# Two groups of six hidden chunks by seven products for eight in the first block, and the rotary tables built early and kept in DRAM

## The chip, the cores and the metric

The kernel runs on one core of one Trainium2 chip. The metric is the device time in microseconds (us) of one execution. The engines are named as in the profile: PE is TensorE (PEld its weight loads), DVE VectorE, ACT ScalarE, POOL GpSimd, SP SyncE, which here only issues DMAs.

## The reference

One encoder layer in float32: 512 tokens, model width 1024, hidden width 2816 (22 chunks of 128).

```python
def swiglu(h, w_in, w_out):
    gate, up = jnp.split(h @ w_in, 2, axis=-1)
    return (jax.nn.silu(gate) * up) @ w_out
# Per layer:
#   x += 1/2 * g1 * SwiGLU_1(mod(RMSNorm(x)))
#   x += g2 * W_out( sig(gA) * W_A(WindowGQA+sink) + sig(gB) * W_B(DiffAttn) )
#   x += 1/2 * g3 * SwiGLU_2(mod(RMSNorm(x)))
# shift, scale and g of each line: adaLN columns computed from c
```

The queries and keys of both mixers are rotated by the cosines and sines of `positions * inv_freq` (`rope_tables`). The change concerns the first line (SwiGLU_1, "the first block"), the step from it to the second, and the place where the rotary tables are made.

## The kernel before

**Products.** The residual x lies transposed, as eight row tiles of 128 model columns by 512 tokens (`x_78` to `x_85`, row tiles 0 to 7). Each float32 operand is split into a high part and a low part, and each product is three matmuls (high x high, high x low, low x high; `mm3`, L179 to L181, or `two`, L463 to L465). A weight is loaded into a `raw` buffer (a ring of five), ScalarE casts its high part, VectorE subtracts to get its low part (`split_from`, L195), and both stand in one of five places of a ring until TensorE has used them.

**Seven for eight.** Where the kernel works "by sevens", a product of two matrices that are each cut two by two is made from seven smaller products of sums of the parts, in place of eight. A `Unit` holds such a set: its seven are called s1, a11, a12, s2, s3, s4, a22, and its products have 256 columns (half of the tokens). Its sums of weights are made by DMA accumulations on POOL's queue or by VectorE, and its results are combined by VectorE (L541 to L551). The first block's incoming products go by sevens from hidden pair `PLAIN` = 3 on.

**Outgoing products of the first block.** The 22 hidden chunks leave in sets given by `CHUNKS`: 0 to 5 plain, 6 to 11 by sevens (`SEVEN = (1,)`, two units of `out_unit1`, updates at L1001), 12 to 15 plain, 16 to 21 plain and final. A plain set (`Out1`) goes row tile by row tile: for each, its chunks' products of 512 columns add up in one bank, and VectorE adds the bank, times the gate column g1, to x (L1073). In the final set ScalarE then squares the new x and VectorE adds the square to a sum (`Norm.add`, L309 and L315), for the root mean square of the next norm.

**The boundary.** The last `LAST_1` = 4 row tiles of the final set are made by halves of the tokens (256 columns) in `boundary`, from L386 on: first all four first halves, each followed by its update and `Norm.add`; then the second halves, and among them, at steps that `TO_MIX` counts, the sums of squares of the first half (`Norm.close`, two groups of small matmuls at L348: first of the running sum, then of the last row tile's square alone), the norm's factor and its spread over partitions (L327, L328, L337), and the input of the gates (L359, L360, L368). Then come the first gates' products for the first half, the second half's sums of squares (L348 again), and so on. A step is one chunk's three matmuls; `TO_MIX[0]` = 4 steps of the second half stand before the close, `TO_MIX[2]` = 2 steps of the gates before the second half's sums.

**What sets the order.** Each engine runs its instructions in one written order. On PE, DVE and ACT in the boundary that order is the one in which the code is written, but for what is told to stand behind another instruction (`issue_after`) or is put in by the scheduler where it sees room. SP and POOL run their DMA issues in written order. Modulation columns (`column`, on DVE L288) are spread over the items of the first block by rates (`AHEAD_OF`, `BEHIND`, and 0 in the sevens groups' own items), and loads of 0.5 MB come with them.

**The rotary tables.** A row of parameters is loaded beside the unit behind the sevens group (`load_row`, `by[-1]`). Behind the first block's last items the angles are computed (L1224 to L1241), then the sines; sixteen products (L1268 to L1271) make eight tables: those of the first mixer (`late`) are written to DRAM, those of the second (`soon`) stay in a raw buffer.

**The gates' weights.** `load_split` loads three gate weights of 128x1024 into raw buffers (L222); their casts on ACT and their low parts on DVE (128x1024, L195) fall into the boundary.

## Time and profile before

| | us |
|---|---|
| median of 3 runs | 1031.42 |
| lowest, highest | 1030.89, 1032.16 |
| the profiled execution | 1030.95 |
| its span | 1029.2 |
| PE busy in it | 1023.9 |
| DVE busy | 804.4 |
| ACT busy | 593.8 |
| POOL busy | 168.7 |

A row of a timeline gives the start, the duration, the engine, the line, the operation, what is written and read, and the shape; in brackets stands the idle time just before it and what ended it. A row of the groups of waits gives who waited for what: us in total, times, the longest. A row of busy time by window gives the window, its width, and then the busy time of PE, PEld, DVE, ACT and POOL with their instruction counts, the granted clock of TensorE, the share of the DMA engines' time and GB/s. Buffer numbers are left out of the profile's names. The profile's line numbers are those of the kernel before; in the order of instructions of the changed kernel the same code has the numbers L180 to L182 (products), L196 (splits), L228 (low parts of the gates' weights), L391 (update of a half), L314 and L320 (square and its addition), L332 (norm's factor), L1154 (update of a plain set).

### The profile page before, as it was taken

What the parts mean: (1) busy time and instruction counts of PE and PEld (TensorE: products, weight loads), DVE (VectorE), ACT (ScalarE), POOL (GpSimd) and SP (SyncE); (2) the same over time, 40 slices, a digit from 0 to 9 for tenths busy, and PEclk for the clock granted to TensorE, in tenths of its full rate; (3) what the DMA queues carried; (4) which work ended last, traced back from release to release, by engine and by line L of the source; (5) the groups of instructions that cost most, each with busy time, mean ns of one, the idle gap of its engine ahead of it and who ended that gap; (6) DMA issues with size and microseconds to landing.
All of it is one profiled execution on the core that took longest, in us unless ns stands there. A gap on an engine that the chain in (4) does not pass through costs nothing.

```text
span 1029.2 us, 19174 instructions
## 1 busy us (share of the span) xinstructions
PE 1023.9 (99%) x7454; PEld 950.0 (92%) x7454; DVE 804.4 (78%) x1508; ACT 593.8 (58%) x1040; POOL 168.7 (16%) x197
## 2 busy tenths in 40 slices
PE   9999999999999999999999999999999999999998
PEld 7889899999998988899878888989999999999998
DVE  7887868778878879859772688976898777877877
ACT  6755336553454533768795866534877546655553
POOL 1101011211100100543322101001112112212210
PEclk9999999999999999999999999999999999999999
DMA  9968888998957369696637935974498998999874
GB/s 361 371 192 202 292 220 207 222 227 259 244 153 245 134 259 409 220 274 136 165 83 193 275 120 176 344 243 106 101 237 196 242 231 209 224 223 219 208 156 114
DMA packets 71388, 223.57 MB, mean 217 GB/s; under 512 B 8576, under 2 KB 13312, under 8 KB 71296
## 3 DMA queue, kind: packets, MB, share of 16 engines
q1 hardware_dynamic: 47808, 146.52, 39.4%
q0 software_dynamic: 20352, 71.32, 37.5%
q10 hardware_dynamic: 3136, 4.51, 1.2%
q8 instruction: 58, 0.95, 0.4%
q14 instruction: 34, 0.28, 0.1%
HBM read 212.09 MB, written 10.23 MB: 216 GB/s over the span
## 4 chain that ended last, share of the span: by engine, by line
PE 96%; DVE 2%; ACT 1%; issue 0%; DVEq 0%; ACTq 0%
PE acc L463 7%; PE acc L465 7%; PE acc L464 7%; PE sc L463 7%; PE sc L465 7%; PE sc L464 7%; PE acc L179 5%; PE acc L180 5%; PE acc L181 5%; PE sc L180 4%; PE sc L179 4%; PE sc L181 4%; PE tp L1445 2%; PE sc L192 2%; PE acc L714 2%; PE sc L714 2%
## 5 line engine op out<-in xcount | busy, mean ns | idle before, releaser
L195 ACT CAST high<-raw 128x1024 fp32r<-128x1024 f32 (+2 forms) x176 | 159.0, 914 | 137.7 <-PE acc L464 32.4
L195 DVE TENSOR_TENSOR low<-raw,high 128x1024 fp32r<-128x1024 f32 (+2 forms) x176 | 183.7, 1051 | 42.7 <-ACT high L195 41.7
L463 PE MATMUL acc<-b,high 128*128 128x256 f32 x542 | 150.2, 277 | 0.0
L464 PE MATMUL acc<-b,high 128*128 128x256 f32 x542 | 149.9, 277 | 0.1
L465 PE MATMUL acc<-b,low 128*128 128x256 f32 x542 | 149.9, 277 | 0.0
L464 PE MATMUL sc<-b,high 128*128 128x256 f32 x534 | 147.5, 276 | 0.0
L463 PE MATMUL sc<-b,high 128*128 128x256 f32 x534 | 147.5, 276 | 0.0
L465 PE MATMUL sc<-b,low 128*128 128x256 f32 x534 | 147.5, 276 | 0.0
L195 DVE TENSOR_TENSOR low<-u,high 128x1024 fp32r<-128x1024 f32 (+1 forms) x79 | 93.3, 1181 | 26.7 <-ACT high L195 25.7
L195 ACT CAST high<-u 128x1024 fp32r<-128x1024 f32 (+1 forms) x79 | 80.4, 1019 | 50.0 <-PE sc L464 14.3
L463 PEld LDWEIGHTS acc<-b,high 128*128 128x128 f32 x542 | 101.8, 188 | 0.6 <-DVE f L543 0.3
L464 PEld LDWEIGHTS acc<-b,high 128*128 128x128 f32 x542 | 101.8, 188 | 0.4 <-DVE b L2033 0.3
L465 PEld LDWEIGHTS acc<-b,low 128*128 128x128 f32 x542 | 101.8, 188 | 0.1
L463 PEld LDWEIGHTS sc<-b,high 128*128 128x128 f32 x534 | 100.3, 188 | 0.0
L465 PEld LDWEIGHTS sc<-b,low 128*128 128x128 f32 x534 | 100.3, 188 | 0.0
L464 PEld LDWEIGHTS sc<-b,high 128*128 128x128 f32 x534 | 100.2, 188 | 0.0
L179 PE MATMUL acc<-b,high 128*128 128x512 f32 (+1 forms) x240 | 89.1, 371 | 0.0
L181 PE MATMUL acc<-b,low 128*128 128x512 f32 (+1 forms) x240 | 86.5, 361 | 0.0
L180 PE MATMUL acc<-b,high 128*128 128x512 f32 (+1 forms) x240 | 86.5, 360 | 0.0
L179 PE MATMUL sc<-b,high 128*128 128x512 f32 (+1 forms) x224 | 78.7, 351 | 0.0
L180 PE MATMUL sc<-b,high 128*128 128x512 f32 (+1 forms) x224 | 78.5, 350 | 0.0
L181 PE MATMUL sc<-b,low 128*128 128x512 f32 (+1 forms) x224 | 78.4, 350 | 0.0
(411 smaller groups left out, 2739.1 us busy)
## 6 DMA issues: line engine op xcount, KB each, us to landing
u<-w_mod SPq DMA_DIRECT2D x38, 512.0 KB, 8.4
b<-w_mod SPq DMA_DIRECT2D x32, 512.0 KB, 5.1
raw<-w2i SPq DMA_DIRECT2D x31, 512.0 KB, 5.7
u<-w2i POOLq DMA_DIRECT2D x31, 512.0 KB, 7.0
raw<-w1u SPq DMA_DIRECT2D x24, 512.0 KB, 7.6
u<-w1u POOLq DMA_DIRECT2D x24, 512.0 KB, 8.3
raw<-w_gate SPq DMA_DIRECT2D x16, 512.0 KB, 5.8
low<-w_gate POOLq DMA_DIRECT2D x13, 512.0 KB, 7.2
```

Of the source, the lines that this page charges most:

```text
L179: PE.matmul(out, wh, xh, start=first, stop=False)
L180: PE.matmul(out, wh, xl, start=False, stop=False)
L181: PE.matmul(out, wl, xh, start=False, stop=last)
L192: last = PE.matmul(out, of[j][a], of[j][b], start=i == 0, stop=i == 2).ins
L195: last = S.copy(hi, src), V.tensor_tensor(lo, src, f(hi), ALU.subtract)
L463: PE.matmul(out, wh[:, s], xh, start=first and j == 0, stop=False, skip_group_check=True)
L464: PE.matmul(out, wh[:, s], xl, start=False, stop=False, skip_group_check=True)
L465: PE.matmul(out, wl[:, s], xh, start=False, stop=last and j == 1, skip_group_check=True)
L714: PE.matmul(out1[i][:, r], w[:, i * P : (i + 1) * P], h[:, r], start=first and r.start == 0, stop=last and r.stop == T, skip_group_check=True,
L1445: PE.transpose(tp[:, j * P : (j + 1) * P], src, ident)
```

## The change

The chunks 12 to 17 leave as a second group by sevens, in place of four of them in a plain set and two in the final set, and the final set has four chunks. Five row tiles instead of four are made by halves in the boundary. Modulation columns get a rate in the sevens groups' items (`AMONG`), and places of the ring of weights are moved (`KICKS_1`). One step of the gates more stands before the second half's sums. The row is loaded at row tile 0 of the first plain set, and `tables()` is called at its row tile 1; both halves of the tables go to DRAM, issued by ACT, and `soon` is loaded back by SP ahead of the gates' weights. The low parts of the gates' weights are no longer issued with their casts: they stand in a list, `gate_lows`, and `boundary` issues one behind each update but the first.

```diff
@@ -106,11 +106,11 @@
 
 MIX_ASIDES = 0, 0, 0, 0, 0, 0, FIRST, ASIDE
 
-CHUNKS = (range(0, 6), range(6, 12), range(12, 16), range(16, 22))
-PLAIN, LAST_1 = 3, 4
-
-
-SEVEN, AHEAD_OF, BEHIND = (1,), (0.75, 0.4), (0.5, 0.25)
+CHUNKS = (range(0, 6), range(6, 12), range(12, 18), range(18, 22))
+PLAIN, LAST_1 = 3, 5
+
+
+SEVEN, AHEAD_OF, BEHIND, AMONG = (1, 2), (0.75, 0.4), (0.5, 0.25), (0.18, 0.18)
 
 
 EARLY, NEXT, LATER = 3, 3, 4
@@ -127,9 +127,10 @@
 
 BY_DMA = (5, 7)
 
-KICKS = (3, 5, 7)
-
-TO_MIX = (4, 13, 2, 2, 4, 2, 1)
+ROW_AT, TABLES_AT = 0, 1
+KICKS, KICKS_1 = (3, 5, 7), {6: "s3", 7: "s3", 9: "s3", 10: "s2"}
+
+TO_MIX = (4, 13, 3, 2, 4, 2, 1)
 TO_FFN2 = (3, 1, 2, 2, 3, 2, 1)
 
 PARTS = (range(0, 4), range(4, 8), range(8, 11))
@@ -213,14 +214,18 @@
         for i in [i for i in holders if holders[i] == holder]:
             del holders[i]
 
-    def load_split(src, n=1024, spare=False, aside=0):
+    def load_split(src, n=1024, spare=False, aside=0, due=None):
         raw = sbuf("raw", [P, 1024], F32, RAW)
         if spare:
             hi, lo = (u4().rearrange("p a b -> p (a b)") for _ in range(2))
         else:
             hi, lo = high_low(aside=aside)
         nc.sync.dma_start(raw[:, 0:n], src)
-        split_from(hi[:, 0:n], lo[:, 0:n], raw[:, 0:n])
+        if due is None:
+            split_from(hi[:, 0:n], lo[:, 0:n], raw[:, 0:n])
+        else:
+            S.copy(hi, raw)
+            due.append(lambda: V.tensor_tensor(lo, raw, f(hi), ALU.subtract))
         return hi, lo
 
     HALVES = (slice(0, 2 * P), slice(2 * P, T))
@@ -374,7 +379,7 @@
         hl = [t[2 + c // 4][:, c % 4, :] for c in range(NC)]
         return hh, hl
 
-    def boundary(parts, g, norm, sc, sh, hh, hl, into, ahead, at):
+    def boundary(parts, g, norm, sc, sh, hh, hl, into, ahead, at, due=()):
 
 
 
@@ -383,8 +388,9 @@
 
         def update(m, po, r):
             xr = x[m][:, r]
-            V.scalar_tensor_tensor(xr, po, modv[g][:, m : m + 1], xr, ALU.mult, ALU.add)
+            end = V.scalar_tensor_tensor(xr, po, modv[g][:, m : m + 1], xr, ALU.mult, ALU.add).ins
             norm.add(m, r)
+            return end
 
         def run(steps, n=None):
             for i, _ in enumerate(steps):
@@ -405,10 +411,13 @@
             yield
 
         with tc.manual_schedule(engines=BOUND):
-            for m, products in parts:
+            for i, (m, products) in enumerate(parts):
                 po = bank("sc")[:, 0 : 2 * P]
                 run(products(po, ra))
-                update(m, po, ra)
+                end = update(m, po, ra)
+                if due and i > 0:
+                    with tc.issue_after(end):
+                        due.pop(0)()
             n = 0
             for m, products in parts:
                 po = bank("sc")[:, 0 : 2 * P]
@@ -903,12 +912,14 @@
         u.p, u.in_order = p, ("s2", "s4")
         if p - 1 in by_sevens:
             u.in_order = ("s1", "s2", "s3", "s4", "a22")
-            if p not in by_sevens:
+            if 2 * p in [CHUNKS[i].stop for i in SEVEN]:
                 u.MAKE = dict(Unit.MAKE, s4=1)
         if p == PLAIN:
             u.asides = {"s1": FIRST}
         elif 2 * p in [CHUNKS[i].stop for i in range(len(CHUNKS) - 1) if i not in SEVEN] or p == PLAIN + 1:
             u.asides = {"s2": FIRST}
+        if p in KICKS_1:
+            u.asides = {KICKS_1[p]: FIRST}
         return u
 
     act = {}
@@ -1011,9 +1022,79 @@
     def load_row():
         rows.append(u4(F32).rearrange("p a b -> p (a b)")[:, 0:NROW])
         nc.sync.dma_start(rows[0], a["row"].partition_broadcast(P))
-        rows.append(split[1])
+
+    NF = HD // 2
+    table_scr, soon_scr = (tc.dram_tile([P, 1024], F32, name=nm) for nm in ("table_scr", "soon_scr"))
+    sink = keep([P, 8], "sink")
+
+    def four(t):
+        return [t[:, i * 2 * P : (i + 1) * 2 * P].rearrange("p (t d) -> p t d", t=NT) for i in range(4)]
+
+    def tables():
+        row = rows[0]
...
+        late = u4(F32).rearrange("p a b -> p (a b)")
+        soon = u4(F32).rearrange("p a b -> p (a b)")
+
...
+        S.dma_start(table_scr, late)
+        S.dma_start(soon_scr, soon)
...
+    by[-2] = lambda: (iter(()), 0, tables)
 
     def eighth(u):
         def steps():
@@ -1162,18 +1243,16 @@
                 for m in range(2):
                     item1(out, m, ks=range(len(chunks) - 2, len(chunks)))
             for m in range(2 if final else 0, NC - LAST_1 if final else NC):
-                item1(out, m, n=rate[0])
+                item1(out, m, *({ROW_AT: (-1,), TABLES_AT: (-2,)}.get(m, ()) if chunks is CHUNKS[0] else ()), n=rate[0])
             return out
 
         for v, nxt in zip(order, order[1:] + [None]):
             if v.p - 1 in by_sevens or v not in units1.values():
-                rate = 0.0, 0.0
+                rate = 0.0, 0.0 if 2 * v.p in [CHUNKS[i].stop for i in SEVEN] and v in units1.values() else AMONG[v not in units1.values()]
             else:
                 rate = AHEAD_OF if v.p <= by_sevens[0] else BEHIND
             n = rate[1]
             due = [v.p - 1] if v in units1.values() and v.p - 1 in by else []
-            if v.p - 2 in by_sevens and v.p - 1 not in by_sevens and v in units1.values():
-                due.append(-1)
             if v is order[0]:
                 item1(v, "s1", n=n)
                 item1(v, "a11", n=n)
@@ -1206,78 +1285,12 @@
 
 
 
-    row = rows[0]
     V.tensor_scalar(sub8, par[:, SUBLN : SUBLN + 1], 1.0 - LAM_INIT, None, ALU.mult)
 
-    NF = HD // 2
...
     table = {}
-    late = u4(F32).rearrange("p a b -> p (a b)")
     soon = sbuf("raw", [P, 1024], F32, RAW)
-
...
-    table_scr = tc.dram_tile([P, 1024], F32, name="table_scr")
-    G.dma_start(table_scr, late)
...
+    nc.sync.dma_start(soon, soon_scr)
+    table["qb"], table["kb"] = (four(soon)[i : i + 2] for i in (0, 2))
@@ -1315,7 +1328,8 @@
         S.activation(t, out, AF.Tanh, scale=0.5)
         S.dma_start(gate_scr[j], t)
 
-    gate_w = [load_split(a["w_gate"][j], spare=True) for j in range(3)]
+    gate_lows = []
+    gate_w = [load_split(a["w_gate"][j], spare=True, due=gate_lows) for j in range(3)]
     gate_out = {}
 
     def first_gates(r):
@@ -1335,7 +1349,7 @@
     vb_w = boundary(
         last1, G1, n2, SC2, SH2, hh, hl, first_gates,
         lambda: [load_split(a["w_vb"][j]) for j in range(4)],
-        TO_MIX,
+        TO_MIX, gate_lows,
     )
     for j in range(3):
         gate_end(j, gate_out[j])
```

The body of `tables()` is the code that stood behind the block; it is left out here, but for its last lines.

In the boundary, VectorE's order before, from the end of the tables to the norm's factor (`sink` is the tables' last copy, `sc` a bank of products, `f_261` the running sum of squares, `u_284`, `u_287`, `u_290` the gates' low parts):

```order
L1277 COPY sink<-u_205_2314 128x2x4
L386 SCALAR_TENSOR_TENSOR x_82<-sc_3470,mod_90,x_82 128x256
L315 TENSOR_TENSOR f_261_3308<-f_261_3308,f_292_3490 128x256
L386 SCALAR_TENSOR_TENSOR x_83<-sc_3493,mod_90,x_83 128x256
L195 TENSOR_TENSOR u_284_3452<-raw_3450,u_283_3451 128x1024
L315 TENSOR_TENSOR f_261_3308<-f_261_3308,f_294_3513 128x256
L386 SCALAR_TENSOR_TENSOR x_84<-sc_3516,mod_90,x_84 128x256
L195 TENSOR_TENSOR u_287_3458<-raw_3456,u_286_3457 128x1024
L315 TENSOR_TENSOR f_261_3308<-f_261_3308,f_296_3536 128x256
L386 SCALAR_TENSOR_TENSOR x_85<-sc_3539,mod_90,x_85 128x256
L195 TENSOR_TENSOR u_290_3464<-raw_3462,u_289_3463 128x1024
L327 TENSOR_SCALAR sm_3579<-tp_3574 128x2
```

And now, from the last wide update's neighbourhood on (`x_81` is row tile 3, `u_294`, `u_297`, `u_300` the gates' low parts):

```order
L391 SCALAR_TENSOR_TENSOR x_81<-sc_3678,mod_90,x_81 128x256
L320 TENSOR_TENSOR f_277_3591<-f_277_3591,f_302_3692 128x256
L391 SCALAR_TENSOR_TENSOR x_82<-sc_3695,mod_90,x_82 128x256
L320 TENSOR_TENSOR f_277_3591<-f_277_3591,f_304_3709 128x256
L228 TENSOR_TENSOR u_294_3663<-raw_3661,u_293_3662 128x1024
L391 SCALAR_TENSOR_TENSOR x_83<-sc_3713,mod_90,x_83 128x256
L320 TENSOR_TENSOR f_277_3591<-f_277_3591,f_306_3727 128x256
L228 TENSOR_TENSOR u_297_3668<-raw_3666,u_296_3667 128x1024
L391 SCALAR_TENSOR_TENSOR x_84<-sc_3731,mod_90,x_84 128x256
L320 TENSOR_TENSOR f_277_3591<-f_277_3591,f_308_3745 128x256
L228 TENSOR_TENSOR u_300_3673<-raw_3671,u_299_3672 128x1024
L391 SCALAR_TENSOR_TENSOR x_85<-sc_3749,mod_90,x_85 128x256
```

There are five updates in place of four, each addition to the sum of squares stands next behind its update, and the low parts stand behind the additions; the tables are gone.

ScalarE's order in the same place before (`u_283`, `u_286`, `u_289` are the gates' high parts, `f_292` and so on squares):

```order
L309 ACTIVATE f_267_3374<-x_81 128x512
L309 ACTIVATE f_292_3490<-x_82 128x256
L195 CAST u_283_3451<-raw_3450 128x1024
L309 ACTIVATE f_294_3513<-x_83 128x256
L195 CAST u_286_3457<-raw_3456 128x1024
L309 ACTIVATE f_296_3536<-x_84 128x256
L195 CAST u_289_3463<-raw_3462 128x1024
L309 ACTIVATE f_298_3559<-x_85 128x256
```

And now:

```order
L314 ACTIVATE f_280_3623<-x_80 128x512
L227 CAST u_293_3662<-raw_3661 128x1024
L227 CAST u_296_3667<-raw_3666 128x1024
L314 ACTIVATE f_302_3692<-x_81 128x256
L227 CAST u_299_3672<-raw_3671 128x1024
L314 ACTIVATE f_304_3709<-x_82 128x256
L314 ACTIVATE f_306_3727<-x_83 128x256
L314 ACTIVATE f_308_3745<-x_84 128x256
L314 ACTIVATE f_310_3763<-x_85 128x256
```

The casts of the first two gates' weights now stand ahead of the first half's first square, the third ahead of the second square; before, they stood behind the first, the second and the third square.

The queue of SP before the boundary, first before:

```order
L1039 DMA raw_3378<-w1o 128x768
L1039 DMA raw_3382<-w1o 128x768
L1039 DMA raw_3386<-w1o 128x768
L1039 DMA raw_3390<-w1o 128x768
L222 DMA raw_3450<-w_gate 128x1024
L222 DMA raw_3456<-w_gate 128x1024
L222 DMA raw_3462<-w_gate 128x1024
L222 DMA raw_3775<-w_vb 128x1024
```

And now:

```order
L1120 DMA raw_3627<-w1o 128x512
L1120 DMA raw_3631<-w1o 128x512
L1120 DMA raw_3635<-w1o 128x512
L1120 DMA raw_3639<-w1o 128x512
L1120 DMA raw_3643<-w1o 128x512
L1292 DMA raw_3650<-soon_scr 128x1024
L223 DMA raw_3661<-w_gate 128x1024
L223 DMA raw_3666<-w_gate 128x1024
L223 DMA raw_3671<-w_gate 128x1024
L223 DMA raw_3981<-w_vb 128x1024
```

The final set's weights are 128x512 in place of 128x768, and the fetch of the tables stands ahead of the gates' weights.

108 lines of the change are left out of this document (51 added, 57 removed).

## The prediction

> **What bounds the kernel now.** I read the page's busy times and its chain of waits first, then the busy time by stage, then the instructions of TensorE and VectorE one by one where the first block closes.
>
> ```profile
> span 1029.2 us, 19174 instructions
> PE 1023.9 (99%) x7454; PEld 950.0 (92%) x7454; DVE 804.4 (78%) x1508; ACT 593.8 (58%) x1040; POOL 168.7 (16%) x197
> PE 96%; DVE 2%; ACT 1%; issue 0%; DVEq 0%; ACTq 0%
> ```
>
> TensorE is busy 99% of the span and owns 96% of the chain. A matmul taken away is time won, unless TensorE then waits; so I count its matmuls first and look for new waits after. What one costs is read from the spacing of two starts, not from the durations, which overlap:
>
> ```profile
> 302.03 0.28 PE L463 MATMUL op<-b,high 128*128 128x256 f32 x1
> 304.75 0.28 PE L463 MATMUL acc<-b,high 128*128 128x256 f32 x1
> ...
> 317.84 0.39 PE L179 MATMUL acc<-b,high 128*128 128x512 f32 x1
> 328.04 0.39 PE L179 MATMUL acc<-b,high 128*128 128x512 f32 x1
> ```
>
> From the first row to the second 24 matmuls of 256 columns start: 2.72/24 = 0.1133 us. From the third to the fourth 45 of 512 columns: 10.20/45 = 0.2267 us, just twice as much. So 256 columns carry no surcharge, and work can be counted in columns.
>
> By stage (columns: window, the sum of its width, busy us with instructions of PE, PEld, DVE, ACT and POOL, granted clock, DMA share, GB/s):
>
> ```profile
> 107.00:140.00 33.00, 33.00 (x149) 27.36 (x148) 24.24 (x41) 9.96 (x14) 3.36 (x4) 1.00 0.91 294
> 208.00:224.00 16.00, 16.00 (x143) 16.00 (x143) 12.21 (x19) 9.09 (x12) 2.62 (x3) 1.00 1.01 259
> 245.00:267.00 22.00, 22.00 (x100) 18.21 (x99) 18.47 (x29) 7.14 (x9) 2.62 (x3) 1.00 1.03 308
> 313.00:332.00 19.00, 19.00 (x97) 15.99 (x96) 16.58 (x25) 8.48 (x12) 1.68 (x3) 1.00 0.69 233
> 332.00:341.00 9.00, 9.00 (x79) 8.96 (x78) 8.40 (x29) 3.88 (x7) 1.08 (x2) 1.00 0.48 165
> 341.00:357.00 16.00, 15.70 (x133) 15.44 (x132) 12.34 (x30) 7.58 (x15) 3.63 (x6) 1.00 0.45 161
> ```
>
> These are the first plain outgoing set, the outgoing products of the group by sevens, the plain set of four chunks, the final set, and the boundary (two rows). Only the last shows TensorE short of its window, 0.30 us. Just ahead of that, VectorE is busy 8.40 of 9.00 us: the boundary is where there is no room.
>
> **TensorE's saving.** Six plain chunks cost 6 x 8 x 3 = 144 matmuls of 512 columns, 32.64 us. By sevens the counts of the two programs give 252 of 256 columns, 28.55 us: seven eighths. The later row tile that moves into the boundary only changes its shape (12 of 512 become 24 of 256). In all +252 and -24 of 256 columns, -132 of 512: 28.55 - 2.72 - 29.92 = **-4.09 us**.
>
> **The work beside it.** The sevens group already made shows what a second one asks: VectorE 12.21 of 16 us, 76%, with TensorE full. The plain chunks that it replaces had VectorE at 18.47 of 22, 84%. The modulation columns now spread over the groups, by the program's rates, fall into idle time of this kind:
>
> ```profile
> 212.62 1.23 DVE L195 TENSOR_TENSOR low<-raw,high 128x1024 fp32r<-128x1024 f32 x1 [1.41 <-ACT high L195]
> ```
>
> I cost the group at nothing. Its cover is that idle time, and the bound above is what a late weight costs there: DMA is full there (1.01), and more modulation columns mean more loads.
>
> ```profile
> ACT high L195 <- DMA u<-w1q: 2.4, 2, 1.3
> ```
>
> A cast waited 1.3 us for an outgoing weight at worst. One such wait passed on to TensorE would be 0 to 1.3 us.
>
> The tables: sixteen products at 0.20 us, some fifteen instructions for the angles, and the two sums and the copy, some 6.5 us of VectorE, move to the first plain set. The window 107 to 140 has 33.00 - 24.24 = 8.8 us idle there, so they fit on the sum. A late update delays only a bank that is needed two row tiles on. Nothing to 1 us; I take nothing. Writing the tables to DRAM and fetching half of them back is 1.5 MB, 5 us at the 308 GB/s of the table above; it is awaited only where the gates begin. By itself the move wins nothing on TensorE, which has no wait there that it would remove.
>
> **The boundary.** This is the term that decides. Here is VectorE before, around the last wide update (332.42) and the four narrow ones, and then TensorE's two sums of squares:
>
> ```profile
> 328.93 0.96 DVE L195 TENSOR_TENSOR low<-raw,high 128x768 fp32r<-128x768 f32 x1
> 329.80 0.68 DVE L315 TENSOR_TENSOR f<-f,f 128x512 f32<-128x512 f32 x1
> 330.40 1.28 DVE L288 CUSTOM_DVE_ANT_0 b<-b,ka,par 128x1024 f32<-128x1024 f32 x1
> 331.61 0.29 DVE L1268 TENSOR_TENSOR u<-u,u 128x128 f32<-128x128 f32 x1
> 332.42 0.74 DVE L1073 SCALAR_TENSOR_TENSOR x<-acc,mod,x 128x512 f32<-128x512 f32 x1
> 333.08 0.28 DVE L1268 TENSOR_TENSOR u<-u,u 128x128 f32<-128x128 f32 x1
> 336.47 0.48 DVE L386 SCALAR_TENSOR_TENSOR x<-sc,mod,x 128x256 f32<-128x256 f32 x1
> 337.43 0.43 DVE L315 TENSOR_TENSOR f<-f,f 128x256 f32<-128x256 f32 x1 [0.49 <-ACT f L309]
> 337.77 0.48 DVE L386 SCALAR_TENSOR_TENSOR x<-sc,mod,x 128x256 f32<-128x256 f32 x1
> 338.37 1.23 DVE L195 TENSOR_TENSOR u<-raw,u 128x1024 fp32r<-128x1024 f32 x1
> 339.51 0.42 DVE L315 TENSOR_TENSOR f<-f,f 128x256 f32<-128x256 f32 x1
> 339.85 0.48 DVE L386 SCALAR_TENSOR_TENSOR x<-sc,mod,x 128x256 f32<-128x256 f32 x1
> 341.71 0.48 DVE L386 SCALAR_TENSOR_TENSOR x<-sc,mod,x 128x256 f32<-128x256 f32 x1
> ...
> 343.40 0.16 DVE L327 TENSOR_SCALAR sm<-tp 128x2 f32<-128x2 f32 x1
> ...
> 341.85 0.61 PE L348 MATMUL tp<-ones,f 128*128 128x2 f32 x4
> 342.75 0.61 PE L348 MATMUL tp<-ones,f 128*128 128x2 f32 x4 [0.30 <-ACT f L309]
> ```
>
> Two things are to be seen. The tables' products (331.61 to 336.47) made VectorE late, and it caught up enough that TensorE lost only about half a microsecond: its first sums start at 341.85 and hold it for about 0.35 (an estimate: three spacings of 256 columns), the last start at 342.75, so 0.55 us are lost. And where an addition follows its own update directly, as at 336.47 and 337.43, it waits for ScalarE's square in between, so that the pair costs 1.30 us (336.47 to 337.77); with a gate weight's low part in between, as from 337.77 to 339.85, the wait is covered.
>
> After the change VectorE's order is update, addition, update, addition, low part, update, addition, low part, and so on: every addition stands directly behind its update, and all three low parts stand uncovered between the pairs. From the end of TensorE's plain set, VectorE has: start 0.13, update of row tile 2 0.66 (332.42 to 333.08), a low part of 512 columns 0.60 (scaled from 0.87 for 768, 328.93 to 329.80), a modulation column 1.21 (330.40 to 331.61), a wide addition 0.60 (329.80 to 330.40): 3.20. Then four pairs of 1.30 = 5.20, three low parts of 1.14 (338.37 to 339.51) = 3.42, and the last update with its square until TensorE can start, 1.04 (341.71 to 342.75). Together 12.86 us.
>
> TensorE has five halves of twelve products and the first twelve of the second half, 72 x 0.1133 = 8.16 us, and 0.35 for the first sums: 8.51. It loses 12.86 - 8.51 = 4.35 us in place of 0.55: **+3.80**. The pause is in pieces. The last addition ends at 12.86 - 1.04 - 1.14 = 10.68, where TensorE wants it at 8.16: 2.5 us, of which some 0.6 fall earlier, on a product whose bank the third update has not read. The other 1.8 lie ahead of the last sums. All of TensorE's program is queued behind it.
>
> After that the second half's sums come closer:
>
> ```profile
> 347.56 0.87 DVE L359 SCALAR_TENSOR_TENSOR f<-x,mod,tp 128x256 f32<-128x256 f32 x2
> 351.38 0.48 DVE L386 SCALAR_TENSOR_TENSOR x<-sc,mod,x 128x256 f32<-128x256 f32 x1
> 352.40 0.43 DVE L315 TENSOR_TENSOR f<-f,f 128x256 f32<-128x256 f32 x1 [0.54 <-ACT f L309]
> ...
> 352.88 0.61 PE L348 MATMUL op<-ones,f 128*128 128x2 f32 x4
> ```
>
> Before, the addition at 352.40 ends just as the sums start, 10.13 us after 342.75. Now VectorE has, from the last sums on: 0.65 to its first step (343.40) and 0.08 in it, three pairs of 1.30 (TensorE's 12 products each, 1.36, hold them up by some 0.1), the nine steps of gate input of before (347.56 to 351.38, 3.82), and an update with the end of its addition (351.38 to 352.83, 1.45): 10.0. TensorE has three products fewer on that way, 10.13 - 0.34 = 9.8. **+0.2** (0 to 0.5).
>
> ScalarE: two gate casts of 1.03 us now stand ahead of the first square, and one ahead of the second.
>
> ```profile
> 337.31 1.03 ACT L195 CAST u<-raw 128x1024 fp32r<-128x1024 f32 x1
> ...
> 323.06 3.97 SPq L222 DMA_DIRECT2D raw<-w_gate  x3
> raw<-w_gate SPq DMA_DIRECT2D x16, 512.0 KB, 5.8
> ```
>
> Their loads wait for buffers that the final set's low parts free, about 4 us later than the 323 of before, behind the fetch of the tables. The tables' fetch and the first two gate weights, 1.5 MB at 308 GB/s, take 5 us from about 327, so that the second cast ends near 333. The first square is due at about 334.7: the plain set ends near 331.0 (341.85, less 2.72 us of products saved by then, less 8.16), and 3.20 and an update follow. Nothing if so; if the second is issued only near 329 and takes the page's 5.8 us, its cast ends at 335.8, 1.1 us late, and the chain of pairs shifts with it. The w1o loads ahead of them are half as many as before, so I take **0** (0 to 1.1).
>
> **Sum.** -4.09 + 3.80 + 0.20 + 0 = -0.09 us. The profiled execution took 1030.95 us (1.75 around its span), which gives 1030.86; the median of the runs is 0.47 above it, and the same step from the median gives 1031.3.
>
> **Rivals.**
> (a) *The boundary swallows less.* If the waits between update and addition close (0.96 to 0.6, four times 0.3) and the modulation column has gone by before, VectorE is 1.2 + 1.2 us earlier, and the loss is 1.4 in place of 3.8: 1028.9. With no loss at all it is -4.09, 1027.3. For it speaks that the order of a program tells a time only with every wait known; against it, that the rows at 337.43 and 352.40 show the very wait, 0.49 and 0.54.
> (b) *Weights come late in the second sevens group (slower).* The place is the outgoing products of that group. DMA stands at 1.01 in the first one, and in the second the outgoing weights, their accumulations on POOL's queue and modulation loads, which the first did not have, share it. Two uncovered waits of the 1.3 kind, with the 0.5 that the second half's sums may cost at most in place of 0.2, add 2.9: 1034.2. It decides from about 2.1 us of lost time. Against it: but for the modulation loads the first group has the same traffic, and TensorE lost nothing.
> (c) *The pause costs clock (slower).* The granted clock is 1.00 in every window, and the longest wait of TensorE in this trace is 0.9 us. A pause of 4.35 us is outside what it shows. Were the products after it to run at double spacing for as long, that would lose 2.2 us: 1033.5. The Trainium skill, page "TensorE: Matmul & The Clock Gate", section "What's actually happening", says that an idle window of about 3.4 us halves the clock; no run here shows it. By that rule the pieces, the longest about 2 us with matmuls between, would stay under it.
> (d) *The casts hold the first square up by the full 1.1 us*: 1032.4, inside no change.
>
> ```profile
> PE acc L639 <- DVE sm L645: 0.9, 1, 0.9
> ```
>
> **Chances.** Forecast 0.46, (a) 0.27, (b) 0.13, (c) 0.05, (d) 0.09. What can be told from no change here is 0.2%, 2.06 us: below 1029.4 or above 1033.5. All of (a) and a little of the forecast's lower edge lie below (0.29), (d) and most of the forecast between (0.49), (b), (c) and the forecast's upper edge above (0.22). The forecast's own range is 1029.5 to 1033.3; for eight in ten it takes in most of (a) and (b): 1028.0 to 1034.2.
>
> **What would show it.** Right: in the changed kernel TensorE waits some 4 us in all between the boundary's halves and its last sum of squares, on VectorE and ScalarE; VectorE runs there without idle time but about 0.5 us ahead of each addition; the second half's sums start near 353.8 (352.88, less 27 products, 3.06, and 4.0 of waits more); no wait over 0.5 us in the second sevens group or the first plain set. Wrong: TensorE waits under 2 us at the close (then (a)), or for a cast of an outgoing weight between 225 and 310 (then (b)), or a granted clock below 1.00 after the close (then (c)).

## The result, and the profile after

| | us |
|---|---|
| the changed kernel, median (lowest, highest) | 1054.34 (1052.97 to 1055.67) |
| the kernel before, beside it | 1031.47 (1030.89 to 1032.16) |
| ratio | 1.0221, interval 1.0204 to 1.0239 |
| predicted | 1031.3 (1028.0 to 1034.2) |

The change makes the kernel slower by 22.9 us, far outside the range. The profiled execution took 1052.97 us, its span 1051.2, which is 22.0 more than before. The page of the changed kernel opens:

```profile
span 1051.2 us, 19466 instructions
PE 1030.4 (98%) x7550; PEld 955.9 (91%) x7550; DVE 820.4 (78%) x1557; ACT 603.6 (57%) x1068; POOL 175.2 (17%) x204
```

TensorE looks as full as before, and this is the first lesson: its busy time went up by 6.5 us although it has work for 4.09 us less. At a granted clock of 0.50 a matmul keeps TensorE busy for nearly twice the time: from 134.18 to 136.31 us of the changed kernel the starts of products of 512 columns are 0.43 us apart, at 1.00 they are 0.23 us apart. So the stages tell more than the shares. These are the first matmuls of the stages in TensorE's timeline of the changed kernel: first plain set, sevens groups with their plain neighbours, final set, boundary, and the end of the first gates.

```profile
107.99 0.50 PE L180 MATMUL sc<-b,high 128*128 128x512 f32 x1 [0.28 <-ACT high L196]
152.86 0.28 PE L472 MATMUL acc<-b,high 128*128 128x256 f32 x1
338.71 0.40 PE L181 MATMUL acc<-b,high 128*128 128x512 f32 x1
346.31 0.29 PE L180 MATMUL sc<-b,high 128*128 128x256 f32 x1
389.49 0.40 PE L1380 MATMUL sc<-high,b 128*128 128x512 f32 x1
```

In the kernel before, the same matmuls start at 107.01, 139.69, 316.68, 332.12 and 369.56 (the last one is the end of the last gate product). With the columns counted as in the prediction:

| stretch | before | after | difference | by the count of columns | lost |
|---|---|---|---|---|---|
| up to the first plain set | 107.01 | 107.99 | +0.98 | 0 | 0.98 |
| first plain set | 32.68 | 44.87 | +12.19 | 0 | 12.19 |
| sevens groups and what lies between | 176.99 | 185.85 | +8.86 | +6.79 | 2.07 |
| final set | 15.44 | 7.60 | -7.84 | -8.16 | 0.32 |
| boundary to the end of the gates | 37.44 | 43.18 | +5.74 | -2.72 | 8.46 |
| all that follows | 659.64 | 661.71 | +2.07 | 0 | 2.07 |

The last column is what is left over the count; it sums to 26.1 us, and 26.1 - 4.09 = 22.0. That the count holds is seen in the final set, which is 7.84 us shorter where 8.16 are counted. The 0.98 us ahead of the first plain set can't be put down to the change: 0.74 of them are a wait 7.75 us after the start, where `dve_only` (below), which has none of the change, waits for 1.0 us, and `unit_in_b8`, which has all of it, reaches the set at 107.00. Most of the loss lies in two places, and the groups of TensorE's waits name them:

```profile
PE sc L180 <- ACT high L196: 4.9, 3, 2.6
PE sc L180 <- DVE x L391: 3.1, 2, 1.6
PE sc L182 <- DVE low L196: 1.9, 3, 0.8
PE tp L353 <- DVE f L320: 1.7, 1, 1.7
PE tp L353 <- ACT f L314: 1.4, 1, 1.4
```

The first and the third row lie in the first plain set, but for 0.28 us just ahead of it (casts and low parts of outgoing weights came late), the others in the boundary. Together 6.8 and 6.2 us: not enough for 12.19 and 8.46. Most of the rest is the clock. The busy times by window of the changed kernel (the seventh figure behind the window, without the counts in brackets, is the granted clock):

```profile
107.99:152.86 44.87, 38.30 (x144) 29.54 (x145) 32.53 (x73) 10.90 (x17) 3.53 (x4) 0.89 0.74 238
133.00:134.00 1.00, 1.00 (x4) 0.81 (x5) 0.98 (x2) 0.00 (x0) 0.00 (x0) 0.81 1.05 427
136.00:137.00 1.00, 1.00 (x4) 0.81 (x3) 0.00 (x0) 0.00 (x0) 0.00 (x0) 0.50 1.05 283
144.00:146.00 2.00, 2.00 (x6) 1.54 (x5) 1.96 (x5) 0.00 (x0) 0.00 (x0) 0.50 1.05 178
363.00:364.00 1.00, 1.00 (x5) 1.00 (x6) 0.55 (x2) 0.36 (x1) 0.76 (x2) 0.50 0.87 320
366.00:367.00 1.00, 1.00 (x11) 1.00 (x10) 0.46 (x2) 0.42 (x1) 0.38 (x1) 1.00 0.00 0
```

Within the first plain set some 10 us ran at 0.50 (134 to 137 and 141 to 147, with their edges), which loses about 5; in the boundary some 3.4 us (362.3 to 365.7).

**Why casts came late in the first plain set.** SP's timeline, of the changed kernel and then of the kernel before:

```profile
115.48 0.33 SPq L255 DMA_DIRECT2D b<-w_mod  x1
124.88 0.33 SPq L506 DMA_DIRECT2D u<-w1u  x1
125.30 0.38 SPq L1120 DMA_DIRECT2D raw<-w1o  x1
```

```profile
111.63 0.33 SPq L250 DMA_DIRECT2D b<-w_mod  x1
112.01 0.42 SPq L497 DMA_DIRECT2D u<-w1u  x1
112.52 0.38 SPq L1039 DMA_DIRECT2D raw<-w1o  x1
```

SP issued nothing for 9.4 us. The load `u<-w1u` goes into a buffer of a ring of six (`u4`) that `tables()` also draws from, and by the program's semaphores it waits for the one in which sines and cosines lie. VectorE's last table product frees that buffer; it stands at 124.57 in VectorE's timeline, 0.31 us before the load is issued:

```profile
124.57 0.28 DVE L1087 TENSOR_TENSOR u<-u,u 128x128 f32<-128x128 f32 x1
```

Behind the waiting load in SP's queue stand the outgoing weights that the plain set itself needs. ScalarE's casts then wait for DMA, and TensorE for the casts (2.10 us at 131.90 and 2.56 us at 141.00):

```profile
131.02 0.83 ACT L196 CAST high<-raw 128x768 fp32r<-128x768 f32 x1 [3.73 <-DMA raw<-w1o]
139.17 1.04 ACT L196 CAST high<-u 128x1024 fp32r<-128x1024 f32 x1 [7.32 <-DMA u<-w1u]
```

**The boundary.** VectorE, and then ScalarE, at the first two half updates of the changed kernel:

```profile
349.59 0.48 DVE L391 SCALAR_TENSOR_TENSOR x<-sc,mod,x 128x256 f32<-128x256 f32 x1
352.66 0.42 DVE L320 TENSOR_TENSOR f<-f,f 128x256 f32<-128x256 f32 x1 [2.59 <-ACT f L314]
353.00 0.48 DVE L391 SCALAR_TENSOR_TENSOR x<-sc,mod,x 128x256 f32<-128x256 f32 x1
354.71 0.43 DVE L320 TENSOR_TENSOR f<-f,f 128x256 f32<-128x256 f32 x1 [1.23 <-ACT f L314]
357.15 0.43 DVE L320 TENSOR_TENSOR f<-f,f 128x256 f32<-128x256 f32 x1 [0.48 <-ACT f L314]
```

```profile
349.69 1.05 ACT L227 CAST u<-raw 128x1024 fp32r<-128x1024 f32 x1 [1.76 <-DMA raw<-w_gate]
351.26 1.05 ACT L227 CAST u<-raw 128x1024 fp32r<-128x1024 f32 x1 [0.52 <-DMA raw<-w_gate]
352.22 0.41 ACT L314 ACTIVATE f<-x 128x256 f32<-128x256 f32 x1
```

The first square could have begun at 350.0; two gate casts that wait for their weights stand ahead of it, and it begins at 352.22. The first two additions wait 2.59 and 1.23 us where 0.48 is the plain wait between update and addition. The last sums of squares start at 362.10, 15.8 us after the plain set's end.

### The profile page after: what moved, and what is told of

Same layout as the page of the kernel before. It is cut to its first block, busy times and chain, and to the rows that moved or that the text cites. A ratio compares the mean times of both kernels' runs of the same rounds, so it can differ in the third digit from the quotient of the medians.

```text
span 1051.2 us, 19466 instructions
## 1 busy us (share of the span) xinstructions
PE 1030.4 (98%) x7550; PEld 955.9 (91%) x7550; DVE 820.4 (78%) x1557; ACT 603.6 (57%) x1068; POOL 175.2 (17%) x204
## 4 chain that ended last, share of the span: by engine, by line
PE 84%; DVE 6%; DMA 5%; ACT 3%; issue 1%; POOL 0%; SPq 0%; DVEq 0%; ACTq 0%; POOLq 0%
PE acc L472 7%; PE acc L473 7%; PE acc L474 7%; PE sc L472 7%; PE sc L473 7%; PE sc L474 7%; PE acc L180 4%; PE acc L181 4%; PE acc L182 4%; PE sc L182 2%; PE sc L180 2%; PE sc L181 2%; PE acc L723 2%; PE sc L193 2%; PE sc L723 2%; PE tp L1459 1%
## 5 line engine op out<-in xcount | busy, mean ns | idle before, releaser
L196 ACT CAST high<-raw 128x1024 fp32r<-128x1024 f32 (+2 forms) x176 | 158.9, 913 | 124.5 <-PE acc L473 32.7
L472 PE MATMUL acc<-b,high 128*128 128x256 f32 x576 | 159.8, 278 | 0.4 <-DVE f L552 0.2
L473 PE MATMUL acc<-b,high 128*128 128x256 f32 x576 | 159.5, 277 | 0.1
L474 PE MATMUL acc<-b,low 128*128 128x256 f32 x576 | 159.4, 277 | 0.0
L472 PE MATMUL sc<-b,high 128*128 128x256 f32 x568 | 157.2, 277 | 0.7 <-ACT f L550 0.7
L473 PE MATMUL sc<-b,high 128*128 128x256 f32 x568 | 157.0, 276 | 0.0
L474 PE MATMUL sc<-b,low 128*128 128x256 f32 x568 | 157.0, 276 | 0.0
L472 PEld LDWEIGHTS acc<-b,high 128*128 128x128 f32 x576 | 108.1, 188 | 1.3 <-DVE f L552 0.6
L473 PEld LDWEIGHTS acc<-b,high 128*128 128x128 f32 x576 | 108.2, 188 | 0.3 <-DVE b L2047 0.3
L474 PEld LDWEIGHTS acc<-b,low 128*128 128x128 f32 x576 | 108.3, 188 | 0.1
L472 PEld LDWEIGHTS sc<-b,high 128*128 128x128 f32 x568 | 106.7, 188 | 0.9 <-ACT f L550 0.9
L473 PEld LDWEIGHTS sc<-b,high 128*128 128x128 f32 x568 | 106.6, 188 | 0.0
L180 PE MATMUL acc<-b,high 128*128 128x512 f32 (+1 forms) x228 | 84.4, 371 | 0.0
L181 PE MATMUL acc<-b,high 128*128 128x512 f32 (+1 forms) x228 | 81.7, 359 | 0.0
L180 PE MATMUL sc<-b,high 128*128 128x512 f32 (+1 forms) x184 | 66.9, 363 | 8.0 <-ACT high L196 4.9
L182 PE MATMUL sc<-b,low 128*128 128x512 f32 (+1 forms) x184 | 66.2, 360 | 1.9 <-DVE low L196 1.9
L181 PE MATMUL sc<-b,high 128*128 128x512 f32 (+1 forms) x184 | 65.9, 358 | 0.0
```

Of the source, the lines that this page charges most:

```text
L180: PE.matmul(out, wh, xh, start=first, stop=False)
L181: PE.matmul(out, wh, xl, start=False, stop=False)
L182: PE.matmul(out, wl, xh, start=False, stop=last)
L196: last = S.copy(hi, src), V.tensor_tensor(lo, src, f(hi), ALU.subtract)
L472: PE.matmul(out, wh[:, s], xh, start=first and j == 0, stop=False, skip_group_check=True)
L473: PE.matmul(out, wh[:, s], xl, start=False, stop=False, skip_group_check=True)
```

## The experiments

Each is compared with the kernel before, timed beside it (1031.2 to 1031.5 us). The theory after the two traces was: (A) the tables' place in VectorE's order holds up one load, and SP's queue stands still behind it. The rivals: the second sevens group itself costs the time; or VectorE has too little time for the tables there.

**Which half of the change costs.** The changed kernel with the tables where they stood before (their code behind the block, the row loaded beside the unit behind the sevens group):

```diff
-    by[-2] = lambda: (iter(()), 0, tables)
...
-                item1(out, m, *({ROW_AT: (-1,), TABLES_AT: (-2,)}.get(m, ()) if chunks is CHUNKS[0] else ()), n=rate[0])
+                item1(out, m, n=rate[0])
...
+            if v.p - 2 in by_sevens and v.p - 1 not in by_sevens and v in units1.values():
+                due.append(-1)
```

> The changed kernel with the rotary tables made where the kernel before made them (angles and products behind the first block, the second mixer's tables kept in a raw buffer); chunks, boundary and all else as changed. Theory A (the early tables occupy buffers of the ring that the incoming units' loads use, SP waits for one of them and the outgoing weights queue behind it): the first plain set goes back to 32.7 us for its 144 products from 44.9, and the loss of 13.2 us there is gone; the table products are back on VectorE in the boundary, which adds 0 to 5 us there. 1041 to 1047. Rival B (the loss comes from the second sevens group and its modulation columns, not from the tables): the first plain set stays at 44 or so, 1052 to 1056.

Measured 1045.47 us, ratio 1.0129 (1.0114 to 1.0145). The first plain set takes 32.7 us again (107.56 to 140.24): what it lost came with the tables. But the time falls by only 9 us, since the tables now collide with what the rest of the change has put at the block's end, where at most 0.55 us was lost before:

```profile
PE sc L180 <- DVE x L391: 3.2, 1, 3.2
PE acc L472 <- DVE f L552: 2.4, 1, 2.4
```

The angles stand ahead of a sum that closes the sevens group (2.4 us), the table products, 339.82 to 343.05, ahead of the first half update (3.2 us), and the clock is half for 3.4 us behind each, and for 6.8 us from 351.9 on, around the last sums of squares. So this kernel does not show what the sevens group costs by itself.

The counterpart, the kernel before with only the tables moved (diff: the hunks on `ROW_AT`, `tables()` and `soon` of the change, and nothing else):

> The kernel before with only the tables moved to the first plain set and kept in DRAM. Theory A: the first plain set loses 12 to 14 us as in the changed kernel, the boundary loses nothing new; 1042 to 1046. Rival B (sevens group and columns): within 2 us of before. Rival C (VectorE's 6.5 us of work alone): the same as A here, told apart by the run with private work.

Measured 1043.55 us, ratio 1.0115 (1.0100 to 1.0130). The first plain set takes 45.6 us (107.44 to 153.01), with waits of 7.0 us for casts; the sevens group and the final set after it keep their lengths (176.98 and 15.44 us). The move of the tables alone costs 12 us.

**Is it the place?** The changed kernel with the tables two row tiles later:

```diff
-ROW_AT, TABLES_AT = 0, 1
+ROW_AT, TABLES_AT = 0, 3
```

> The changed kernel with one number changed: the tables are called at row tile 3 of the first plain set in place of row tile 1. The unit's load into the shared ring is then issued ahead of the tables, and none of the eight outgoing weights stands behind a load that waits for them. Theory A: the loss in the first plain set falls from 13.2 us to under 3; 1041 to 1046, unless the next unit's load, which now waits for the tables, is late. Rival C (VectorE's work): VectorE has as much to do there, 1051 to 1055. Rival D (DMA traffic of the row and the tables): as C.

Measured 1055.78 us, ratio 1.0228 (1.0206 to 1.0250). The first plain set is short again (107.58 to 140.77, 33.2 us), but nothing is won: SP's queue stood still later and longer.

```profile
134.43 0.33 SPq L255 DMA_DIRECT2D b<-w_mod  x1
153.69 0.33 SPq L506 DMA_DIRECT2D u<-w1u  x1
```

This time 19.3 us, until VectorE's last table product at 153.38; here the profile's waits of SP name it, 18.9 us for the table products at L1087. The sevens group that follows pays, with waits of 3.0, 2.1 and 1.8 us and three stretches at half the clock. The stall follows the tables.

**VectorE's time, or its order?** The kernel before, with 35 operations of 128x128 (a memset and 34 additions, some 7 us of VectorE at the 0.20 us of a table product), whose result is not used; there are no tables in it, and no load of this stage goes into the ring that their buffer is taken from:

```diff
+    def extra():
+        d = f2()[:, 0:P]
+        V.memset(d, 0.0)
+        for _ in range(34):
+            V.tensor_tensor(d, d, d, ALU.add)
...
+                item1(out, m, *((-2,) if chunks is CHUNKS[0] and m == 1 else ()), n=rate[0])
```

> The kernel before with 35 more VectorE instructions of 128x128 (about 7 us, as much as the tables) issued at row tile 1 of the first plain set, on a buffer that no load uses; the tables stay where they were, and the result of the added work is not used. Theory A: within 1 us of before, first plain set 32.7 to 33.5 us. Rival C: VectorE's time is what delays the plain set, 8 to 13 us more than before.

Measured 1047.38 us, ratio 1.0156 (1.0141 to 1.0171). That is the number of the rival: work on VectorE alone, on a buffer that no load waits for, costs as much. The trace shows that SP's queue stands still here too, on another load:

```profile
106.98 0.83 SPq L1046 DMA_DIRECT2D raw<-w1o  x1
128.04 0.33 SPq L250 DMA_DIRECT2D b<-w_mod  x1
```

```profile
126.53 0.28 DVE L1020 TENSOR_TENSOR f<-f 128x128 f32<-128x128 f32 x1
126.73 1.28 DVE L288 CUSTOM_DVE_ANT_0 b<-b,ka,begin 128x1024 f32<-128x1024 f32 x1
127.93 0.08 DVE L288 DVE_READ_ACCUMULATOR2_ANT mod<- 128x1 f32 x1
```

A modulation load (`b<-w_mod`) needs the buffer that the modulation column at 126.73 reads. That column stands behind the added work in VectorE's order, so the load is issued at 128.04, after 21 us without one; the outgoing weight behind it follows at 128.94, where the kernel before issues it at 112.52. Theory (A) was too narrow: the shared buffer is one way for it, the order on VectorE the general one. If the total time were what counts, the same work in pieces would cost the same. So seven pieces of five operations, at row tiles 1 to 7:

```diff
-        for _ in range(34):
+        for _ in range(4):
...
-                item1(out, m, *((-2,) if chunks is CHUNKS[0] and m == 1 else ()), n=rate[0])
+                item1(out, m, *((-2,) if chunks is CHUNKS[0] and m > 0 else ()), n=rate[0])
```

> The kernel before with the same 35 added VectorE instructions as dve_only, but in seven pieces of five, one at each of row tiles 1 to 7 of the first plain set, on private buffers. Theory (what cost 16 us in dve_only was not VectorE's time but that the added work came ahead of the modulation columns in VectorE's order, and SP's queue stood still behind a column's load): columns slip by a microsecond or so, SP issues on, 0 to 2 us over before. Rival (7 us more of VectorE's work in this stage cannot be hidden): 8 us or more over before.

Measured 1031.17 us, ratio 0.9998 (0.9988 to 1.0007): nothing. Its first plain set by window:

```profile
107.00:140.00 33.00, 33.00 (x149) 27.36 (x148) 29.07 (x68) 9.81 (x14) 3.50 (x4) 1.00 0.92 294
```

VectorE is busy 29.07 of 33.00 us, where the kernel before has 24.24, and TensorE loses nothing. 28 of the 35 operations run in this window, the other seven just ahead of it, from 102.1 us on. The time was there, as the prediction had it; 16 us hung on where in the order it was taken.

**The one load.** The changed kernel, with the waiting weight in a buffer of another ring (`b8`), so that it does not wait for the tables:

```diff
+        if p == 5:
+            u.spare, u.roomy = (), ("s1",)
```

> The changed kernel, but the one incoming unit whose load waited for the tables' buffer gets a buffer of another ring; the tables stay at row tile 1 and VectorE has all of their work. Theory A (SP's queue stands still behind a load that waits for VectorE's last table product): SP issues on, the 144 products of the first plain set take 32.7 to 34.5 us in place of 44.9 and keep full clock; 1041 to 1043. Rival C (VectorE's time itself makes the updates and low parts late): the plain set stays above 40 us; 1050 to 1055.

Measured 1043.19 us, ratio 1.0114 (1.0099 to 1.0130): 11 us of the 22.9 gone by one buffer. SP issues that load at 114.92:

```profile
114.54 0.33 SPq L255 DMA_DIRECT2D b<-w_mod  x1
114.92 0.42 SPq L506 DMA_DIRECT2D b<-w1u  x1
115.44 0.38 SPq L1122 DMA_DIRECT2D raw<-w1o  x1
```

The first plain set takes 34.4 us (107.00 to 141.35), with one wait left for the first low part (1.03 us), behind the angles on VectorE. All the DMA traffic of the tables is still there, so it is not the traffic that cost the 11 us. The same edit on the kernel with the tables alone:

> The kernel before with only the tables moved (as tables_only), and the one unit's load in a buffer of another ring (as unit_in_b8). Theory A: of the 12 us that tables_only lost, all but the 1 to 2 us that VectorE's work costs at the first products is back; 1032 to 1034. Rival (the early tables cost more in another way, so that the chunks and the boundary of the changed kernel cost less than I think): 1036 or more.

Measured 1034.07 us, ratio 1.0021 (1.0012 to 1.0031): of the 12.3 us, 9.8 were the blocked queue. What is left is the wait for the first low part, 1.7 us by the waits, and under 1 us that was not traced.

**The tables in pieces.** If the place decides, the tables themselves can be cut: the changed kernel, its buffers unchanged, with `tables()` yielding nine times, so that its pieces stand among other work from row tile 2 on:

```diff
-ROW_AT, TABLES_AT = 0, 1
+ROW_AT, TABLES_AT = 0, 2
...
-    by[-2] = lambda: (iter(()), 0, tables)
+    by[-2] = lambda: (tables(), 9, None)
```

> The changed kernel, with one edit: the tables' work is cut into nine pieces that stand between other work of VectorE around row tiles 2 to 5 of the first plain set, in place of one piece at row tile 1. Nothing is left out or added, and the buffers stay as in the change, so the load of an outgoing weight still waits for the last table product. Theory (place in the order, not VectorE's time; SP's queue stands still behind that one load): VectorE's other work and so the other loads are no longer held up, the first plain set ends within 0 to 4 us of its old length (32.4) in place of 44.6, and the time is about 1054.3 - 12 + 2 = 1044 us (1041 to 1047). Rival (the total work of tables and set is too much for VectorE or for DMA there): the set still takes over 40 us and the time stays over 1050.

Measured 1056.63 us, ratio 1.0258 (1.0225 to 1.0290): a miss. The first plain set did what the theory said (107.03 to 140.92, 33.9 us), but the last pieces came to stand behind low parts of the next group's weights, which wait for places in the ring, and the load that waits for the last table product came later still:

```profile
123.93 0.40 SPq L506 DMA_DIRECT2D raw<-w1u  x1
150.51 0.33 SPq L255 DMA_DIRECT2D b<-w_mod  x1
156.40 0.33 SPq L506 DMA_DIRECT2D u<-w1u  x1
```

SP issues nothing for 26.6 us, until the modulation column at 149.25, behind the first eight table products, is done, and then for 5.9 us until the last product. TensorE pays in the sevens group with waits of 3.6, 2.1 and 1.8 us. Pieces are good where nothing waits for the last one. Here something did.

**The boundary.** Starting from `unit_in_b8`, the gates' casts are moved behind the updates together with their low parts, so that no cast holds up the first square:

```diff
-            S.copy(hi, raw)
-            due.append(lambda: V.tensor_tensor(lo, raw, f(hi), ALU.subtract))
+            due.append(lambda: split_from(hi, lo, raw))
```

> As unit_in_b8, and the casts of the three gates' weights are issued with their low parts, behind the second, third and fourth update, in place of ahead of the first two squares. Theory of the boundary (ScalarE's casts, which wait for late loads, hold up the first two squares by 2.1 and 0.75 us, VectorE's additions with them, and the pauses then cost clock): 2 to 4 us less than unit_in_b8. Rival (VectorE's own chain is as long anyway, the casts only fill its waits): within 0.7 us of unit_in_b8.

Measured 1043.45 us, ratio 1.0118 (1.0099 to 1.0137), against 1043.19 without the edit: no gain. The wait moved along the chain:

```profile
PE tp L352 <- DVE f L319: 2.3, 1, 2.3
PE tp L352 <- ACT f L313: 2.0, 1, 2.0
PE sc L180 <- DVE x L390: 1.1, 1, 1.1
```

The low parts on VectorE, 3.42 us in the prediction, now stand behind the casts. So two of the three low parts go to ScalarE and DMA (the negated high part, to which POOL's queue adds the weight), the third behind the last update:

```diff
+                def far():
+                    S.activation(lo, raw, AF.Identity, scale=-1.0)
+                    G.dma_start(lo, src, accum_op=ALU.add)
```

> As unit_in_b8, and two of the gates' three low parts are made by ScalarE (minus the rounded high part) and a DMA that adds the weight, the third by VectorE behind the last update. VectorE's chain up to the last sum falls by 3.4 us, to 9.4 against TensorE's 8.5. Theory (VectorE's chain sets the close): TensorE waits 1 to 2 us at the close in place of 6.2, clock stays full: 5 to 8 us less than unit_in_b8. Rival (ScalarE becomes the chain, with six more operations of 1 us among the squares, or the low parts land after the first gate products): 0 to 3 us less, with TensorE waiting at the close for ScalarE or behind it for the low parts.

Measured 1040.50 us, ratio 1.0082 (1.0066 to 1.0098). The close itself is as short as before: the first sums of squares start at 345.22, the last at 346.12, 9.5 us after the plain set's end at 336.58. That is 2.7 us less than `unit_in_b8`, and not the 5 to 8 of the theory: the low parts land late, as the rival had it, and the gates wait for them and run at half the clock for 3.4 us:

```profile
PE acc L182 <- DMA u<-w_gate: 1.7, 1, 1.7
```

With the gates' loads ahead of the fetch of the tables and the first low part begun at once:

```diff
-    soon = sbuf("raw", [P, 1024], F32, RAW)
-    nc.sync.dma_start(soon, soon_scr)
...
+    gate_w = [load_split(a["w_gate"][j], spare=True, due=gate_lows, first=j == 0) for j in range(3)]
+    soon = sbuf("raw", [P, 1024], F32, RAW)
+    nc.sync.dma_start(soon, soon_scr)
```

> As lows_by_dma, but the gates' weights are loaded ahead of the tables' fetch, the first gate's low part is begun ahead of the first square and the second's three updates earlier than there, so that the DMA that completes it is issued some 2 to 3 us earlier. Theory (what lows_by_dma still loses behind the close is the late low part, 2.0 us of waiting and as much of half clock): 3 to 5 us less than lows_by_dma, 1035 to 1038, no wait for a gate's low part, full clock. Rival (the low parts' DMAs are slow because the next weights' loads share the DMA engines, and land as late): within 1.5 us of lows_by_dma.

Measured 1036.42 us, ratio 1.0045 (1.0030 to 1.0061). The boundary to the end of the gates takes 35.5 us (336.58 to 372.04; before 37.44, and 34.72 by the count of columns), at full clock:

```profile
336.00:350.00 14.00, 13.40 (x112) 12.99 (x111) 10.78 (x23) 8.62 (x15) 4.46 (x7) 1.00 0.98 316
```

It is still slower than the kernel before: 0.7 us are lost ahead of the first plain set, 2.4 in it, 1.8 in the sevens groups, 1.0 in the final set, 0.7 in the boundary, and 3.7 after the gates, 1.4 of them in a new wait, 66 us after the gates, for ScalarE's work of a later stage (`PE acc L180 <- ACT f L1495`). Last, the same with the tables in nine pieces:

> All that helped in one kernel: the gates' low parts made early (as in the run before of that name), the buffer for the waiting load taken from another ring, and the tables' work in nine pieces from row tile 2 on. Theory: of the 2.1 us that the first plain set still lost (a wait for the first low part, behind the angles in VectorE's order), 0.5 to 2 go: 1034.5 to 1036 us. The rest (some 2 us of boundary and square sums by the second sevens group, and later drifts of about 3) stays, so that it does not beat the kernel before (1031.5). Rival: the pieces, spread over more row tiles, hold up more low parts than they free, and it is no faster than 1036.4.

Measured 1039.11 us, ratio 1.0077 (1.0061 to 1.0092): slower than whole, so the rival held. VectorE's timeline shows one reason:

```profile
135.74 0.29 DVE L1102 TENSOR_TENSOR u<-u,u 128x128 f32<-128x128 f32 x1 [4.21 <-DMA table_scr<-u]
137.70 0.75 DVE L1173 SCALAR_TENSOR_TENSOR x<-sc,mod,x 128x512 f32<-128x512 f32 x1
```

A table product waits 4.2 us for the store of the first tables, and the plain set's update stands behind it. TensorE waits for that update (1.65 us at 138.59), and the first plain set takes 36.1 us in place of 35.0. The sevens groups lose 2.4 us more than in `low_early`; the waits there, 1.9 and 0.6 us, are for ScalarE's copies of results. No kernel made here beats the one before.

## Why the prediction was wrong, point by point

- **TensorE's saving, -4.09: right as far as the traces show it.** The final set shows 7.84 of the 8.16 us counted there, and the boundary of `low_early`, at full clock, is within 0.7 us of the count; no run has the second sevens group alone.
- **The tables in the first plain set, "nothing to 1 us; I take nothing": the step that failed, 12 us.** It had two reasons. "They fit on the sum" was true: `dve_spread` puts as many operations there at no cost. "A late update delays only a bank that is needed two row tiles on" looked at one follower only. VectorE runs in order, and behind the tables stand also the modulation columns and low parts that free the buffers of SP's next loads; and SP issues in order too. The prediction costed the DMAs beside the tables by their bytes (1.5 MB, 5 us) and never asked what SP's queue waits for. `unit_in_b8` and `tables_only_b8` show that the one load explains 11 of 22.9, and 9.8 of 12.3 us.
- **The sevens group, 0 to 1.3, took 0: undersized.** The changed kernel lost 2.07 us there and `low_early` 1.8; `unit_in_b8`, `casts_behind`, `lows_by_dma` and `early_and_pieces` lost 2.9 to 4.2. In the changed kernel and in `low_early` no late weight stands out there, as rival (b) had it; what the waits show are ScalarE's copies of results (0.7 and 0.9 us, one of each). Why the copies come late was not tried.
- **The boundary's chain of VectorE, +3.80: the mechanism right.** The pairs of 1.30 with a wait of 0.48 stand in the trace, and without the low parts the close takes 9.5 us, where the prediction's 12.86 less 3.42 gives 9.44.
- **ScalarE's casts, "I take 0 (0 to 1.1)", rival (d): undersized.** They cost 2.9 us: the last sums start 15.79 us after the plain set's end in place of 12.86, and the two long waits (2.59 and 1.23, less 0.48 each) make 2.86 of it. The start was right: the fetch of the tables is issued 4.06 us ahead of the plain set's end, where the prediction has 4.0. The 5 us for it and two weights were too few: the rate was taken at 308 GB/s from a stage in full stream; here SP began to issue the three weights at 342.84, behind the fetch, and the first two casts, waiting for them, started only 6.85 and 8.42 us later. `casts_behind` adds that this term does not simply go away, since the low parts need the casts.
- **The clock, rival (c): its sign came true, its chance of 0.05 was too small, and it had one place of two.** A clock below 1.00 behind the close is there, and it took 1.6 us in the boundary, where (c) has 2.2 (27 products behind the close in 4.89 us, before 3.53, and 0.25 in the sums). It took some 5 us more in the first plain set, where the prediction had no pause. The prediction read the Trainium skill's page "TensorE: Matmul & The Clock Gate", section "What's actually happening", as if pieces under its idle window of about 3.4 us were safe. The trace differs: the pieces were 1.4 to 1.7 us here, and 3.4 us at 0.50 followed them. The Trainium skill's same page, section "A second HAM failure mode: psum-queue depth-cycling", says that short idle times, when they come often enough, make the clock go back and forth; with that the trace agrees, by the same 3.4 us.
- **The second half's sums, +0.2: right.** 8.46 lost in the boundary, less 6.73 at the close (15.79 - 8.51 - 0.55) and 1.6 of clock, leaves 0.1.
- **After the gates, nothing expected; 2.07 measured.** By the times of the kernel before, some 0.7 us of it are lost at 420 to 460 (0.3 to 0.5 in `unit_in_b8`, `lows_by_dma` and `tables_in_pieces`, 0.06 in `casts_behind`), and about 1 us at 740 to 780 (0.7 to 1 in `unit_in_b8`, `casts_behind` and `dve_only`, the last without the sevens group). Their cause stays open.

## What to carry to other kernels

When work moves to another place on an engine that runs in order, list what stands behind it there: not only the instruction that the next matmul needs, but each one whose end frees a buffer, and then the queue whose next load waits for that buffer, with everything behind that load. Idle time on the sum says whether the work fits, and says nothing about what it holds up; put it down in small pieces, unless something waits for the last piece. A few microseconds of waits of TensorE are to be priced with the clock: here 6.8 us of them cost 12.19 in one stage, and 6.2 cost 8.46 in another.

## What the runs showed of the hardware

The granted clock falls to 0.50 after pauses of TensorE as short as 1.4 to 2.6 us, and not each time. What tells these apart was not tried in a run of its own, but the traces show a pattern. In the changed kernel the stretches at 0.50 are 133.6 to 137.0, 140.4 to 147.3 and 362.3 to 365.7 us, so 3.4, 6.8 and 3.4 us long, and their starts lie 2 and 67 steps of 3.413 us behind the first. In the eight other kernels that have such stretches they last 3.4 or 6.8 us too (13.65 once, in `tables_at_3`), with starts in steps of the same length. So the clock changes on a fixed grid of some 3.41 us, whose position differs from run to run.

Cut along that grid, between 100 and 450 us, every window at full clock in which TensorE was busy for 46% or less was followed by one at 0.50 (17 windows, busy 9 to 46%). Of those busy for 47 to 57%, three were followed by 0.50 and seven were not; of those above, none was. From 0.50 the clock came back only behind a window busy for 97% or more; windows at 0.50 that were busy for 45 to 89% were followed by another one. So what counts in these traces is the share of a fixed window, and not the length of one pause. A pause of 2.1 us in the changed kernel lies nearly whole in one window (busy 42%) and is followed by half the clock; one of 2.2 us in `tables_only` is divided between two (busy 54 and 74%) and costs only its length. In `dve_only` two pauses of 3.4 us fall into windows busy for 19 and 33%, and 6.8 us at 0.50 begin at the end of each window.
